# Two heads in flight in a gated-delta block: the next head's projection written ahead of a head's chain, and small copies and sums on ScalarE

## The chip, the cores and the metric

The kernel runs on one core of a Trainium2 chip. The metric is the device time of one execution in microseconds (us), the median of several runs. The core has five engines that run their own instruction streams in order and wait for each other by semaphores: TensorE (PE in the rows, its weight loads PEld), VectorE (DVE), ScalarE (ACT), GpSimd (POOL) and SyncE (SP), which issues most DMAs.

## What is computed

A decoder trunk on x of 512 tokens by 1024, with two layers, conditioned by a vector c. The first layer mixes tokens with a gated delta rule in 8 heads of 128, then an MLP; the second makes a shared key and value, and does differential attention and another MLP. The change lies in the first layer's mixer, cut here to what matters:

```
def gated_deltanet(h, w_in, conv_w, a_log, dt_bias, out_g, w_out):
    proj = h @ w_in
    qkv = causal_conv_silu(proj[..., :2 * GDN_HK + GDN_HV], conv_w)     # 4 taps along the tokens
    ...
    o = gated_delta_rule(l2norm(q), l2norm(k), v, g, beta)
    o = rmsnorm(o, out_g) * jax.nn.silu(z)
    return o.reshape(B, S, GDN_HV) @ w_out

def gated_delta_rule(q, k, v, g, beta):   # in chunks
    a_mat = jnp.where(strict, jnp.einsum('bhnik,bhnjk->bhnij', kb, kc) * decay, 0.0)
    rhs = jnp.concatenate([vc * bc[..., None], kb * jnp.exp(gcum)[..., None]], axis=-1)
    sol = lax.linalg.triangular_solve(eye + a_mat, rhs, left_side=True, lower=True, unit_diagonal=True)
    ...
    def step(state, inp):
        v_new = u_i - jnp.einsum('bhck,bhkv->bhcv', w_i, state)
        o_i = jnp.einsum('bhck,bhkv->bhcv', qg_i, state) + jnp.einsum('bhij,bhjv->bhiv', qk_i, v_new)
        state = state * gl_i[..., None, None] + jnp.einsum('bhck,bhcv->bhkv', kd_i, v_new)
        return state, o_i
    _, o = lax.scan(step, s0, xs)
```

## The kernel before

The program is written in a tile framework. It names tiles and pools, and a scheduler turns the written order into one queue for each engine: of what is ready by its model, what was written earlier goes first. So the order of the Python code is a priority, and the queue that results is fixed when the program is built. Names in the rows are those of tiles; `pj`, `pa`, `pi`, `pr` are PSUM banks.

A head h of the mixer has two parts. `proj_head(h)` streams the weights of its q, k and v (L291, `raw`), rounds them on ScalarE to `wh` (L293), takes the remainder `wl` (L284), multiplies three times for each block (L300 to L302, 512 wide), and convolves the result in the tile `cv` (L481 to L485, one pass on ScalarE, three on VectorE, and the SiLU). `gdn(h)` is a generator in three pieces. The first makes the gate's decay (L531, L532), the natural layouts by transposes (L513), the scaled matrix `bq` (L558), and solves it: 16x16 blocks on 32 partitions in fifteen steps on VectorE (L584 and L586, tiles `pr` and `xv`); a DMA to DRAM and back lays the blocks out over 128 partitions (`tc`), from which VectorE makes `t` (L593). TensorE transposes t (L598) to z and doubles the inverse up to 128 in three rounds (L605 to L638), with `um` between (L607 for blocks of 16, L624 for 32 and 64). The second piece is the chain over four chunks of 128 tokens (L670 to L690), where each chunk has `y` (L681), then the state `st`, the residual `r` (L676) of the next chunk, and so on. The third piece normalizes the output `o` (L696 to L702), transposes it (L513) and scales it to `oT` (L705).

For each head, `proj_head(h)` is written first, then two pieces of `gdn(h)`, then the last piece of the head before it. After the eight heads come the gate's projections (L717, L719, in four pairs of heads), the last piece of head 7, the rounding of `oT` (L745, L284) and the output projection. Spread over the weights tiles is a queue of products for the modulation vectors (L189 loads `mw`, L193 multiplies on VectorE), with MWB buffers.

Three sums of squares in each head (`sumsq`, L518 and L520, of k, q and o) are a Square of 128x512 on ScalarE, then a reduction on VectorE.

Of the kernel before, what the change touches and what calls it, by code (L numbers as in the profile page):

```python
# [12 lines left out]
AF = mybir.ActivationFunctionType  # L13
ALU = mybir.AluOpType
AX = mybir.AxisListType
# [6 lines left out]
NT = S // P  # L22
H = 8
# [8 lines left out]
PAD, PAD_W, PAD_R = 416, 0, 96  # L32
MB = 8
AHEAD = 2
MWB = 4
NE = (0, 1, 2, 1, 2, 0, 1, 0)
CV = 9


C_MODB = 0  # L40
# [45 lines left out]
def trunk_kernel(ctx: ExitStack, tc: tile.TileContext, a, outT):  # L86
    nc = tc.nc
    V, G, A, T = nc.vector, nc.gpsimd, nc.scalar, nc.tensor
# [3 lines left out]
    def nm(s):  # L92
        count[0] += 1
        return f"{s}_{count[0]}"

    def open_pool(name, side="left", bufs=1):
        st = ExitStack()
        p = st.enter_context(tc.tile_pool(name=nm(name), bufs=bufs, side=side, reuse_waits="tile"))
        return p, st
# [28 lines left out]
    def big(pool, tag, bufs, dt=F32):  # L128
        return pool.tile([P, S], dt, tag=tag, name=nm(tag), bufs=bufs)

    def col(n, name="c"):
        return tp.tile([P, n], F32, tag=f"{name}{n}", name=nm(name))

    def bank(tag):
        return pools["p"].tile([P, S], F32, tag=tag, name=nm("p" + tag), bufs=pools["n"][tag])
# [4 lines left out]
    def v3(ap, n=P):  # L140
        return ap.rearrange("p (u f) -> p u f", f=n)
# [34 lines left out]
    def cc(base, n=1):  # L176
        return cols[:, base:base + n]
# [7 lines left out]

    def mod_load(c, pool=None, bufs=MWB):
        src = a["mod_wT"][c * P:(c + 1) * P, :] if c < 96 else a["kv_mod_wT"][(c - 96) * P:(c - 95) * P, :]
        w = (pool or c_pool).tile([P, D], F32, tag="mw", name=nm("mw"), bufs=bufs)
        nc.sync.dma_start(w, src)  # L189
        return w  # L190
# [182 lines left out]
    for k in range(KT):  # L373
        n = NE[k]
        sq = acc[n]
        if k >= 3:
            sq = m_pool.tile([P, S], F32, tag=f"sq{n}", name=nm("sq"), bufs=2)
# [17 lines left out]
    def head_weights(h, k0):  # L395
        return weights(lambda t: [(t[:, :, i, :], v_in[:, k0:k0 + 2, i, h * P:(h + 1) * P]) for i in range(3)],
                       [2, 3, P])

    def head_pair(ps, w, k0):
        for j in (1, 0, 2):  # L400
            for k in range(2):
                three(ps[j], w[0][:, k, j], w[1][:, k, j], hh[k0 + k], hl[k0 + k], k0 + k == 0, k0 + k == KT - 1)
# [25 lines left out]
    g_pool, g_st = open_pool("g", "right")  # L428
# [48 lines left out]
    def conv_silu(ps, tile_idx):  # L477

        w = C_CONV + 4 * tile_idx
        acc = big(g_pool, "cv", CV)  # L480
        A.activation(acc, ps, AF.Copy, scale=cc(w + 3))  # L481
        for s in (1, 2, 3):
            V.scalar_tensor_tensor(out=acc[:, s:], in0=ps[:, :S - s], scalar=cc(w + 3 - s), in1=acc[:, s:],
                                   op0=ALU.mult, op1=ALU.add)
        A.activation(acc, acc, AF.Silu)  # L485
        return acc
# [3 lines left out]
    def proj_head(h):  # L490
        if h < 2:
            ps = ph[h]
        else:
            ps = [bank("j") for _ in range(3)]
            for k0 in range(0, KT, 2):
                head_pair(ps, head_weights(h, k0), k0)
        kT[h] = conv_silu(ps[1], 8 + h)
        qT[h] = conv_silu(ps[0], h)
        vT[h] = conv_silu(ps[2], 16 + h)

    def uu(t, n):
        return t[:, n * P:(n + 1) * P]
# [6 lines left out]
    def gdn(h):  # L509
# [4 lines left out]
            return ps  # L514

        def sumsq(src, tag):
            sq = big(g_pool, {"sqq": "sqk"}.get(tag, tag), 1)
            A.activation(sq, src, AF.Square)  # L518
            ss = col(4, tag)
            V.tensor_reduce(out=ss, in_=v3(sq), axis=AX.X, op=ALU.add)  # L520
            return ss


# [14 lines left out]
        kn = big(g_pool, "kn", 3)  # L538
        A.activation(kn, pk, AF.Copy)
        ssk = sumsq(kn, "sqk")  # L540
        V.tensor_scalar(out=ssk, in0=ssk, scalar1=EPS, scalar2=None, op0=ALU.add)
        rk = col(4, "rk")
# [18 lines left out]
        def B(n):  # L561
            return bq[n // 2][:, (n % 2) * 256:(n % 2) * 256 + P]

        def ATT(n):
            return bq[n // 2][:, (n % 2) * 256 + P:(n % 2) * 256 + 256]
# [16 lines left out]
        for s in range(SUB - 1):  # L582
# [4 lines left out]
                            op=ALU.subtract)  # L587
# [15 lines left out]
        pu = bank("i")  # L603
        for n in range(4):
            T.matmul(uu(pu, n), lhsT=B(n), rhs=uu(t_, n), start=True, stop=True)  # L605
        um = big(g_pool, "um", 1)
# [9 lines left out]
        for b in (32, 64):  # L616
            parts = [(slice(lo, lo + b), slice(lo + b, lo + 2 * b)) for lo in ((0, 64) if b == 32 else (0,))]
            pu = bank("i")
            um = big(g_pool, "um", 1)
            for p0, p1 in parts:  # L620
                for n in range(4):
                    T.matmul(pu[p1, n * b:(n + 1) * b], lhsT=B(n)[p0, p1], rhs=uu(t_, n)[p0, p0], start=True, stop=True)
            for p0, p1 in parts:
                V.tensor_copy(um[p1, 0:4 * b], pu[p1, 0:4 * b])  # L624
            pz = bank("i")
            for p0, p1 in parts:
                for n in range(4):
                    T.matmul(pz[p0, n * b:(n + 1) * b], lhsT=um[p1, n * b:(n + 1) * b], rhs=uu(z, n)[p1, p1],
                             start=True, stop=True)
            if b == 32:  # L630
                p0, p1 = parts[0]
                for n in range(4):
                    T.matmul(pz[p1, n * b:(n + 1) * b], lhsT=uu(z, n)[p1, p1], rhs=um[p1, n * b:(n + 1) * b],
                             start=True, stop=True)
                V.tensor_tensor(out=v3(t_)[p1, :, p0], in0=v3(t_)[p1, :, p0],
                                in1=v3(pz[p1, 0:4 * b], b), op=ALU.subtract)
            for p0, p1 in parts:
                V.tensor_tensor(out=v3(z)[p0, :, p1], in0=v3(z)[p0, :, p1], in1=v3(pz[p0, 0:4 * b], b),  # L638
                                op=ALU.subtract)
# [8 lines left out]
        V.tensor_tensor(out=v3(vn), in0=v3(pv), in1=bc(nk, P), op=ALU.mult)  # L648

        ssq = sumsq(natural(qT[h]), "sqq")  # L650
        V.tensor_scalar(out=ssq, in0=ssq, scalar1=float(P), scalar2=EPS * P, op0=ALU.mult, op1=ALU.add)
        rq = col(4, "rq")
# [6 lines left out]
        def out(c):  # L659
            V.tensor_tensor(out=uu(o, c), in0=uu(o, c), in1=R(2), op=ALU.add)  # L660
# [3 lines left out]
        def R(n):  # L664
            return ps[:, n * P:(n + 1) * P]

        for c in range(NT):
            r = uu(vn, 0)
            if c > 0:
                T.matmul(R(3), lhsT=uu(kT[h], c), rhs=st, start=True, stop=True)  # L670
                if c > 1:
                    out(c - 1)
                else:
                    A.activation(uu(o, 0), R(2), AF.Copy)
                r = g_pool.tile([P, P], F32, tag="r", name=nm("r"), bufs=2)
                V.scalar_tensor_tensor(out=r, in0=R(3), scalar=neg[:, c, h:h + 1], in1=uu(vn, c),  # L676
                                       op0=ALU.mult, op1=ALU.add)
                T.matmul(R(1), lhsT=uu(qT[h], c), rhs=st, start=True, stop=True)
            T.matmul(R(2), lhsT=uu(z, c), rhs=r, start=True, stop=True)
            y = g_pool.tile([P, P], F32, tag="y", name=nm("y"), bufs=2)  # L680
            V.tensor_copy(y, R(2))  # L681
            if c < NT - 1:
                T.matmul(R(0), lhsT=uu(kn, c), rhs=y, start=True, stop=True)
            T.matmul(R(2), lhsT=ATT(c), rhs=y, start=True, stop=True)
            if c > 0:
                A.activation(uu(o, c), R(1), AF.Copy, scale=eg[:, c, h:h + 1])
            if c == 0:
                V.tensor_copy(st, R(0))
            elif c < NT - 1:
                V.scalar_tensor_tensor(out=st, in0=st, scalar=gl[:, c, h:h + 1], in1=R(0), op0=ALU.mult, op1=ALU.add)  # L690
        out(NT - 1)

        yield

        so = sumsq(o, "sqo")
        V.tensor_tensor(out=so, in0=so, in1=rq, op=ALU.mult)  # L696
        V.tensor_tensor(out=so, in0=so, in1=rq, op=ALU.mult)
# [14 lines left out]
    def gate(h0, n):  # L712
        ps = proj_T(cols_of(w_in, 3072 + P * h0, P * n), KT, hh, hl, ntile=n)
        for j in range(n):
            h = h0 + j
            sz[h] = big(g_pool, "cv", CV)
            A.activation(sz[h], ps[j], AF.Silu)  # L717
# [8 lines left out]
        queue[c - 17][1].insert(0, lambda c=c: mod_bias(c - 8, c))  # L726
    rate[0] = 0.5
    heads = []
    for h in range(H):
        proj_head(h)  # L730
        heads.append(gdn(h))
        next(heads[h])
        next(heads[h])
        if h:
            next(heads[h - 1], None)
# [275 lines left out]
```

## Time and profile before

| What | Value |
|---|---|
| Median of 3 runs | 1383.1 us (1381.0 to 1383.88) |
| The profiled execution's own time | 1381.92 us |
| Its span in the trace | 1380.1 us |
| TensorE matmul, busy | 1309.7 us, 95% of the span |
| VectorE busy | 850.9 us, 62% |
| ScalarE busy | 529.1 us, 38% |
| GpSimd busy | 471.4 us, 34% |
| Mean granted clock of TensorE | 0.986 of full speed |
| Head 0's first transposes of t (L598) | at 130.2 us |
| Head 7's | at 355.7 us |
| Head 7's output transposes (L513) | at 391.8 us |
| First matmul of the norm behind the mixer | at 416.6 us |

Busy means that an instruction of the engine is running; a wide matmul's end is modelled, so a busy TensorE need not be at its peak. The rows below are from the one execution that was profiled. The last four lines of the table cut the mixer into the stretches that the rows use.

### The profile page before, as it was taken

What the parts mean: (1) busy time and instruction counts of PE and PEld (TensorE: products, weight loads), DVE (VectorE), ACT (ScalarE), POOL (GpSimd) and SP (SyncE); (2) the same over time, 40 slices, a digit from 0 to 9 for tenths busy, and PEclk for the clock granted to TensorE, in tenths of its full rate; (3) what the DMA queues carried; (4) which work ended last, traced back from release to release, by engine and by line L of the source; (5) the groups of instructions that cost most, each with busy time, mean ns of one, the idle gap of its engine ahead of it and who ended that gap; (6) DMA issues with size and microseconds to landing.
All of it is one profiled execution on the core that took longest, in us unless ns stands there. A gap on an engine that the chain in (4) does not pass through costs nothing. (4 is left out here: it accounts for less than half of the span.)

```text
span 1380.1 us, 19204 instructions
## 1 busy us (share of the span) xinstructions
PE 1309.7 (95%) x7240; PEld 1101.4 (80%) x7240; DVE 850.9 (62%) x1688; ACT 529.1 (38%) x951; POOL 471.4 (34%) x281
## 2 busy tenths in 40 slices
PE   4887998999999999999999999999999999999997
PEld 3665787777789888888888987888798888888886
DVE  6989899899846987778861687777552110031113
ACT  3394344443424533225332354444344322143221
POOL 3324132222004544444444012232135444444441
PEclk9997999999999999999999999999999999999998
DMA  9632223225542776776753233222113233233221
GB/s 314 212 90 57 81 78 81 74 72 147 175 151 65 266 239 225 242 236 219 241 165 100 81 100 104 65 66 66 61 62 123 92 96 103 92 100 99 92 76 62
DMA packets 113212, 174.97 MB, mean 127 GB/s; under 512 B 16384, under 2 KB 56992, under 8 KB 113120
## 3 DMA queue, kind: packets, MB, share of 16 engines
q1 hardware_dynamic: 112416, 172.92, 39.5%
q8 instruction: 57, 0.93, 0.3%
q10 hardware_dynamic: 704, 0.83, 0.2%
q14 instruction: 35, 0.29, 0.1%
HBM read 170.04 MB, written 2.62 MB: 125 GB/s over the span
## 5 line engine op out<-in xcount | busy, mean ns | idle before, releaser
L284 POOL TENSOR_TENSOR wl<-raw,wh 128x1024 fp32r<-128x1024 f32 (+1 forms) x137 | 329.3, 2404 | 392.9 <-ACT wh L293 392.9
L293 ACT ACTIVATE wh<-raw 128x1024 fp32r<-128x1024 f32 (+2 forms) x217 | 216.0, 996 | 502.0 <-PE pj L301 250.1
L300 PE MATMUL pj<-h,wh 128*128 128x512 f32 (+1 forms) x816 | 290.9, 360 | 16.0 <-ACT h L278 5.5
L301 PE MATMUL pj<-h,wh 128*128 128x512 f32 (+1 forms) x816 | 292.6, 359 | 0.0
L302 PE MATMUL pj<-h,wl 128*128 128x512 f32 (+1 forms) x816 | 290.4, 358 | 1.1 <-DVE wl L284 1.1
L193 DVE SCALAR_TENSOR_TENSOR mw<-mw,one,cs 128x1024 f32<-128x1024 f32 x96 | 210.1, 2202 | 47.5 <-ACT one L213 47.2
L300 PEld LDWEIGHTS pj<-h,wh 128*128 128x128 f32 x816 | 155.9, 192 | 37.2 <-ACT h L278 7.5
L302 PEld LDWEIGHTS pj<-h,wl 128*128 128x128 f32 x816 | 156.6, 192 | 19.4 <-DVE wl L284 2.4
L301 PEld LDWEIGHTS pj<-h,wh 128*128 128x128 f32 x816 | 156.9, 192 | 17.9 <-DVE h L279 0.3
L301 PE MATMUL pj<-u,wh 128*128 128x512 f32 (+1 forms) x448 | 160.9, 359 | 0.0
L302 PE MATMUL pj<-u,wl 128*128 128x512 f32 (+1 forms) x448 | 160.9, 359 | 0.0
L300 PE MATMUL pj<-u,wh 128*128 128x512 f32 (+1 forms) x448 | 160.8, 359 | 0.0
L346 DVE SCALAR_TENSOR_TENSOR x<-pj,mod,x 128x256 f32<-128x256 f32 (+1 forms) x53 | 30.2, 584 | 152.2 <-PE pj L302 152.2
L284 DVE TENSOR_TENSOR wl<-raw,wh 128x1024 fp32r<-128x1024 f32 (+2 forms) x80 | 84.5, 1058 | 18.7 <-ACT wh L293 18.6
L300 PEld LDWEIGHTS pj<-u,wh 128*128 128x128 f32 x448 | 84.6, 189 | 12.7 <-issue 0.2
L301 PEld LDWEIGHTS pj<-u,wh 128*128 128x128 f32 x448 | 84.6, 189 | 12.5
L302 PEld LDWEIGHTS pj<-u,wl 128*128 128x128 f32 x448 | 84.6, 189 | 12.5
L767 DVE SCALAR_TENSOR_TENSOR pj<-pj,r 128x512 f32<-128x512 f32 x32 | 21.6, 690 | 52.2 <-ACT r L766 52.0
L301 PE MATMUL pn<-h,wh 128*128 128x512 f32 x128 | 49.8, 389 | 0.0
L300 PE MATMUL pn<-h,wh 128*128 128x512 f32 x128 | 49.8, 389 | 0.0
L300 PE MATMUL pm<-h,wh 128*128 128x512 f32 x128 | 49.8, 389 | 0.0
L302 PE MATMUL pm<-h,wl 128*128 128x512 f32 x128 | 49.8, 389 | 0.0
(298 smaller groups left out, 2371.7 us busy)
## 6 DMA issues: line engine op xcount, KB each, us to landing
raw<-in_mlp_w_dram SPq DMA_DIRECT2D x128, 512.0 KB, 3.7
mw<-in_mod_wT_dram SPq DMA_DIRECT2D x96, 512.0 KB, 4.7
raw<-in_a_w_in_dram SPq DMA_DIRECT2D x96, 128.0 KB, 2.6
mw<-in_kv_mod_wT_dram SPq DMA_DIRECT2D x16, 512.0 KB, 5.1
raw<-in_kv_w_dram SPq DMA_DIRECT2D x16, 512.0 KB, 3.3
x<-in_xT_dram SPq DMA_DIRECT2D x16, 256.0 KB, 6.0
raw<-in_a_w_in_dram SPq DMA_DIRECT2D x16, 256.0 KB, 2.9
raw<-in_a_w_out_dram SPq DMA_DIRECT2D x8, 512.0 KB, 4.3
```

Of the source, the lines that this page charges most:

```text
L193: V.scalar_tensor_tensor(out=w, in0=w, scalar=one, in1=cs, op0=ALU.mult, op1=ALU.mult, accum_out=raw_mod[:, c:c + 1])
L284: (V if n else G).tensor_tensor(out=out, in0=x, in1=hi.bitcast(F32), op=ALU.subtract)
L293: A.activation(wh, raw, AF.Copy)
L300: T.matmul(ps, lhsT=wh, rhs=xh, start=first, stop=False, skip_group_check=skip)
L301: T.matmul(ps, lhsT=wh, rhs=xl, start=False, stop=False, skip_group_check=skip)
L302: T.matmul(ps, lhsT=wl, rhs=xh, start=False, stop=last, skip_group_check=skip)
L346: V.scalar_tensor_tensor(out=x[d][:, sl], in0=ps[j][:, sl], scalar=mod[:, gt + d:gt + d + 1], in1=x[d][:, sl], op0=ALU.mult, op1=ALU.add)
L767: V.scalar_tensor_tensor(out=ps[j], in0=ps[j], scalar=0.0, in1=r, op0=ALU.max, op1=ALU.mult)
```

## The change

There are four edits. `proj_head(h + 1)` is now written ahead of `gdn(h)`, so that two heads' q, k and v are held (CV, the buffers of `cv`, goes from 9 to 12, and MWB from 4 to 3). `sumsq` uses four Squares of 128x128 with an accumulator on ScalarE in place of one of 128x512 and a reduction on VectorE. The copies of `um` for blocks of 32 and 64 and those of `y` move from VectorE to ScalarE.

```
-MWB = 4
+MWB = 3
-CV = 9
+CV = 12
...
         def sumsq(src, tag):
-            sq = big(g_pool, {"sqq": "sqk"}.get(tag, tag), 1)
-            A.activation(sq, src, AF.Square)
+            sq = big(g_pool, "sqk", 1)
             ss = col(4, tag)
-            V.tensor_reduce(out=ss, in_=v3(sq), axis=AX.X, op=ALU.add)
+            for c in range(NT):
+                A.activation(uu(sq, c), uu(src, c), AF.Square, accum_out=ss[:, c:c + 1])
             return ss
...
             for p0, p1 in parts:
-                V.tensor_copy(um[p1, 0:4 * b], pu[p1, 0:4 * b])
+                A.activation(um[p1, 0:4 * b], pu[p1, 0:4 * b], AF.Copy)
...
             y = g_pool.tile([P, P], F32, tag="y", name=nm("y"), bufs=2)
-            V.tensor_copy(y, R(2))
+            A.activation(y, R(2), AF.Copy)
...
     heads = []
+    proj_head(0)
     for h in range(H):
-        proj_head(h)
+        if h + 1 < H:
+            proj_head(h + 1)
         heads.append(gdn(h))
         next(heads[h])
         next(heads[h])
```

The queues that the scheduler makes of both programs show where work goes. On TensorE, at the first work on head 7's inverse (L598 of its tile `t`), before had projections of 512 columns (`pj`) between the steps:

```order
L598 MATMUL pi_3231<-mask,t_3229 128x128 x4
L605 MATMUL pi_3238<-t_3229,bq_3167 128x128 x2
L605 MATMUL pi_3238<-t_3229,bq_3168 128x128 x2
L300 MATMUL pj_3656<-h_170,wh_3659 128x512
L301 MATMUL pj_3656<-h_171,wh_3659 128x512
L302 MATMUL pj_3656<-h_170,wl_3661 128x512
L300 MATMUL pj_3655<-h_172,wh_3677 128x512
L301 MATMUL pj_3655<-h_173,wh_3677 128x512
L610 MATMUL pi_3245<-um_3243,z_3236 128x128 x4
L613 MATMUL pi_3250<-z_3236,um_3243 128x128 x4
L302 MATMUL pj_3655<-h_172,wl_3679 128x512
L300 MATMUL pj_3655<-h_174,wh_3677 128x512
```

In the changed program the same steps of head 7 follow one another, behind the last of these projections:

```order
L301 MATMUL pa_3849<-h_3825,wh_3922 128x512
L302 MATMUL pa_3849<-h_3824,wl_3924 128x512
L598 MATMUL pi_3273<-mask,t_3271 128x128 x4
L605 MATMUL pi_3280<-t_3271,bq_3209 128x128 x2
L605 MATMUL pi_3280<-t_3271,bq_3210 128x128 x2
L610 MATMUL pi_3287<-um_3285,z_3278 128x128 x4
L613 MATMUL pi_3292<-z_3278,um_3285 128x128 x4
L622 MATMUL pi_3299<-t_3271,bq_3209 32x32 x2
L622 MATMUL pi_3299<-t_3271,bq_3210 32x32 x2
L622 MATMUL pi_3299<-t_3271,bq_3209 32x32 x2
L622 MATMUL pi_3299<-t_3271,bq_3210 32x32 x2
```

The projections that stood among head 7's steps are ahead of L598. Counted over the whole queue, 512-wide matmuls ahead of head 0's L598 (from the first solve step on) go from 54 to 113, between head 0's and head 7's from 489 to 541, from there to head 7's output transposes from 94 to 0, and behind these, up to the MLP, from 41 to 24.

On VectorE, the stretch up to head 7's `t` (L593) in the program before, with the chain of head 6 ahead of it (`y_2979`, `sqo_3368`):

```order
L284 TENSOR_TENSOR wl_3702<-raw_3698,wh_3700 128x512
L681 COPY y_2979<-pr_2942 128x128
L660 TENSOR_TENSOR o_2941<-o_2941,pr_2942 128x128
L719 TENSOR_TENSOR x_2613<-cv_3649,x_2613 128x512
L520 TENSOR_REDUCE sqo_3368<-sqo_3366 128x4
L696 TENSOR_TENSOR sqo_3368<-sqo_3368,rq_2938 128x4
L697 TENSOR_TENSOR sqo_3368<-sqo_3368,rq_2938 128x4
L698 TENSOR_SCALAR sqo_3368<-sqo_3368 128x4
L284 TENSOR_TENSOR wl_3720<-raw_3716,wh_3718 128x512
L593 TENSOR_TENSOR t_3229<-tc_3227,mask 128x512
L701 TENSOR_TENSOR ro_3373<-ro_3373,rq_2938 128x4
```

And in the changed program, where the steps of head 7's own solve (`xv_3234`) come last before `t_3271`:

```order
L584 TENSOR_TENSOR pr_3235<-mt_3232,xv_3234 32x2x14
L586 TENSOR_TENSOR xv_3234<-xv_3234,pr_3235 32x2x14
L284 TENSOR_TENSOR wl_4041<-raw_4037,wh_4039 128x1024
L584 TENSOR_TENSOR pr_3235<-mt_3232,xv_3234 32x15
L586 TENSOR_TENSOR xv_3234<-xv_3234,pr_3235 32x15
L284 TENSOR_TENSOR wl_4047<-raw_4043,wh_4045 128x1024
L593 TENSOR_TENSOR t_3271<-tc_3269,mask 128x512
L607 TENSOR_TENSOR um_3285<-pi_3280,mask 128x512
L614 TENSOR_TENSOR t_3271<-t_3271,pi_3287 128x512
L615 TENSOR_TENSOR z_3278<-z_3278,pi_3292 128x512
```

The last solve step of head 7 now stands one instruction ahead of its `t`, with the remainder of a weight (`wl`) between.

On ScalarE, in the first head's chain, the program before has roundings of weights (`wh`), the `cv` of the next head, and the outputs of the chain (`o`):

```order
L600 ACTIVATE z_692<-pi_687 128x512
L293 ACTIVATE wh_1862<-raw_1858 128x768
L293 ACTIVATE wh_1888<-raw_1884 128x768
L213 ACTIVATE one_1892<-wh_1888 128x1
L293 ACTIVATE wh_1919<-raw_1915 128x768
L481 ACTIVATE cv_1590<-pj_1474,cols 128x512
L674 ACTIVATE o_779<-pr_780 128x128
L481 ACTIVATE cv_1596<-pj_1473,cols 128x512
L293 ACTIVATE wh_1945<-raw_1941 128x768
L686 ACTIVATE o_779<-pr_780,eg_all 128x128
```

In the changed program the copies `um` and `y` of the same head stand among them, with the Squares of its sum of squares (`sqo_1217`):

```order
L624 ACTIVATE um_734<-pi_733 32x128 x2
L293 ACTIVATE wh_2019<-raw_2015 128x768
L624 ACTIVATE um_762<-pi_761 64x256
L681 ACTIVATE y_804<-pr_802 128x128
L293 ACTIVATE wh_2045<-raw_2041 128x768
L213 ACTIVATE one_2049<-wh_2045 128x1
L674 ACTIVATE o_801<-pr_802 128x128
L520 ACTIVATE sqk_1216,sqo_1217<-o_801 128x128
L681 ACTIVATE y_815<-pr_802 128x128
L686 ACTIVATE o_801<-pr_802,eg_all 128x128
```

The copies and the squares are new in this queue, and each stands behind whatever rounding precedes it. Of 48 rows with moved copies in the whole queue, 10 follow a rounding directly (a row with x2 holds two copies).

## Rows read from the trace of the kernel before

**Rows 1.** Busy time of each engine, granted clock and DMA share by stretch (us).
```profile
core 0: us, PE busy (x) PEld busy (x) DVE busy (x) ACT busy (x) POOL busy (x), PEclk, DMA share, GB/s
86.00:130.00 44.00, 33.35 (x146) 25.67 (x145) 37.35 (x115) 28.05 (x52) 18.25 (x17) 0.81 0.21 55
130.00:355.70 225.70, 213.61 (x1488) 173.81 (x1488) 199.59 (x595) 95.77 (x176) 55.66 (x42) 0.98 0.35 95
355.70:391.80 36.10, 33.14 (x216) 26.24 (x216) 28.69 (x55) 14.45 (x25) 4.24 (x3) 1.00 0.50 159
391.80:416.60 24.80, 24.79 (x157) 22.67 (x158) 12.16 (x20) 6.61 (x11) 0.00 (x0) 0.93 0.45 150
100.00:120.00 20.00, 14.62 (x60) 11.16 (x59) 18.72 (x53) 11.97 (x21) 10.68 (x9) 0.67 0.05 8
500.00:520.00 20.00, 20.00 (x90) 16.58 (x89) 16.42 (x18) 8.28 (x15) 7.28 (x4) 1.00 0.69 229
```

**Rows 2.** Waits of TensorE, 130 to 355.7 us: total, times, longest; ten rows.
```profile
PE pi L598 <- DVE t L593: 5.5, 4, 2.6
...
PE pr L683 <- DVE y L681: 0.2, 1, 0.2
```

**Rows 3.** VectorE groups, 84 to 400 us: busy, mean ns, idle before.
```profile
L193 DVE SCALAR_TENSOR_TENSOR mw<-mw,one,cs 128x1024 f32<-128x1024 f32 x24 | 31.3, 1303 | 0.0
L284 DVE TENSOR_TENSOR wl<-raw,wh 128x768 fp32r<-128x768 f32 x22 | 22.3, 1016 | 0.0
...
L483 DVE SCALAR_TENSOR_TENSOR cv<-pj,cols,cv 128x510 f32<-128x510 f32 x18 | 13.2, 734 | 0.1
...
L681 DVE COPY y<-pr 128x128 f32<-128x128 f32 x32 | 9.0, 283 | 2.8 <-PE pr L679 2.5
...
L520 DVE TENSOR_REDUCE sqo<-sqo 128x4 f32<-128x512 f32 x8 | 5.4, 678 | 1.2 <-ACT sqo L518 1.1
...
L624 DVE COPY um<-pi 32x128 f32<-32x128 f32 x16 | 4.6, 290 | 3.0 <-PE pi L622 2.6
...
L624 DVE COPY um<-pi 64x256 f32<-64x256 f32 x8 | 3.4, 428 | 6.7 <-PE pi L622 6.7
```

**Rows 4.** ScalarE groups, 84 to 400 us, the same columns.
```profile
L518 ACT ACTIVATE sqk<-kn 128x512 f32<-128x512 f32 x8 | 5.0, 624 | 0.1
...
L674 ACT ACTIVATE o<-pr 128x128 f32<-128x128 f32 x8 | 2.2, 275 | 15.1 <-PE pr L670 15.1
```

**Rows 5.** ScalarE's reads of an accumulator in the attention, 860 to 980 us.
```profile
L914 ACT ACTIVATION_READ_ACCUMULATOR on<-po 128x1 f32 x16 | 3.2, 199 | 0.0
```

**Rows 6.** Timeline of TensorE: start us, length us, and idle before.
```profile
155.94 1.06 PE L613 MATMUL pi<-z,um 128*128 128x128 f32 x8
...
391.81 0.66 PE L513 MATMUL pr<-mask,o 128*128 128x128 f32 x4 [2.39 <-POOL o L702]
```

**Rows 7.** Timeline of VectorE, the same columns.
```profile
182.78 0.67 DVE L593 TENSOR_TENSOR t<-tc,mask 128x512 f32<-128x512 f32 x1
...
195.90 0.29 DVE L681 COPY y<-pr 128x128 f32<-128x128 f32 x1
...
306.99 0.27 DVE L681 COPY y<-pr 128x128 f32<-128x128 f32 x1
...
310.60 0.28 DVE L681 COPY y<-pr 128x128 f32<-128x128 f32 x1
...
354.85 0.69 DVE L593 TENSOR_TENSOR t<-tc,mask 128x512 f32<-128x512 f32 x1 [0.72 <-DMA tc<-d]
...
384.30 0.29 DVE L681 COPY y<-pr 128x128 f32<-128x128 f32 x1 [0.82 <-PE pr L679]
```

**Rows 8.** What SyncE's DMA queue waited for, whole span.
```profile
SPq L189 <- DVE mw L193: 88.8, 69, 6.7
```

**Rows 9.** Waits of ScalarE, 84 to 400 us: total, times, longest.
```profile
ACT wh L293 <- PE pj L301: 38.7, 17, 5.2
...
ACT wh L293 <- DMA raw<-in_a_w_in_dram: 24.7, 9, 4.5
```

## The prediction

> **What bounds the kernel now.** I looked first at the share of each engine by stretch, because the change touches only the recurrent block, from 86 us (its first solve step is near) to 416.6 us (the first work of the MLP) [rows 1]. TensorE is busy for 33.35 of 44.00 us before head 0's inverse reaches it (I call this the start), for 213.61 of 225.70 us from head 0's to head 7's (the middle), for 33.14 of 36.10 us in head 7's own chain (the last chain), and for 24.79 of 24.80 us in what is left behind it (the flush). So the block is TensorE's: its queue is long enough that the chains of the heads hide under projection. VectorE is the next one, with 37.35, 199.59 and 28.69 us in the first three stretches. ScalarE has room, with 144.9 us in all four.
>
> The second view is the list of what TensorE waits for in the middle: ten rows from 5.5 to 0.2 us, which add up to 14.3 us [rows 2]. The largest, four waits of 5.5 us together, is for t, the first tile that the solve gives to TensorE; the wait for y is 0.2 us. A faster VectorE can give back in the middle no more than these 14.3 us, whatever is taken from it.
>
> The amount of TensorE's work does not change: both programs issue the same matmuls. What can change is where they stand, thus how much idle time each stretch holds.
>
> **What leaves VectorE and comes to ScalarE.** VectorE loses 32 copies of y (9.0 us), 24 reductions of about 0.68 us (16.3 us) and 24 copies of um (4.6 and 3.4 us), 33.3 us in all [rows 3]. ScalarE gains the copies at its own price for such a tile, 32 x 0.275 = 8.8 us and about 7 us for um. A sum of squares was one pass of 0.624 us there [rows 4]; it becomes four passes of about 0.28, each with a read of the accumulator. Before has such a read elsewhere, at 0.199 us [rows 5], so four passes are 1.9 us, 1.28 more, and 24 of them 30.7 us. ScalarE goes to about 191 of 330 us. A copy takes as long on the one engine as on the other (0.283 and 0.275), so the chain is not shorter by it; only the queue ahead of it differs. I take nothing for that (bounds: a gain up to the 0.2 us wait for y and a loss, which is a rival below).
>
> **The start.** By the order of instructions TensorE has 59 more 512-wide matmuls ahead of head 0's inverse (54 before, 113 now), since head 1's projection stands there, and 8 transposes fewer. One such matmul costs 20.00/90 = 0.222 us in a full stretch [rows 1], a transpose of one block 0.13, as a share of eight fp32 passes of that size in 1.06 us [rows 6]. So TensorE's work in the start is 33.35 + 13.1 - 1.1 = 45.4 us, 1.4 more than the whole stretch of 44.00: the lower bound, +1.4, if no idle is left. VectorE's queue there gains five convolution steps of 0.73, four weight remainders of 1.02 and two modulation products of 1.30 (10.3 us), and loses three reductions (2.0 us) [rows 3]: +8.3 as the upper bound. The order shows that four scalings, six solve steps and three reductions or masks of 0.2 to 1.0 us each also leave it. That takes another 5.5 us or so, an estimate from their number, and I take +2.8.
>
> **The middle.** Between the two inverses the order has 52 more 512-wide matmuls (489 before, 541 now), 8 more transposes and 2 more small matmuls of the decay: 11.5 + 1.1 + 0.4 = 13.0 us. Against it stand the waits of 14.3 us. VectorE's queue from t to t loses 33 us but gains nine weight remainders, three modulation products and the scalings moved in from the start, 198 to 189 us by the same prices. Thus VectorE and TensorE stay near each other head by head, and what TensorE waits for is mostly t. Head 7's t itself waited 0.72 us for a DMA [rows 7], the round trip by which the solved blocks are spread over the partitions. In the new order the solve's last step stands only one instruction ahead of t on VectorE, so this trip is exposed rather than covered. Bounds for the waits that remain: 2 us (all but the transfers vanish) and 14.3 (nothing gained). I take 12, near the upper end, because the largest row ends on a chain through a DMA that no freed VectorE shortens. The middle then gives 13.0 - 2.3 = +10.7.
>
> **The last chain.** Here the cover goes. Before, 94 matmuls of 512 stand in TensorE's queue in it; now none does, and the 72 output matmuls that do not need the last heads stand ahead of head 7's inverse. What is left is the bare chain. Its length I build from the fastest pieces in the trace [rows 7]: t to the first y is 13.1 us for head 2 (182.78 to 195.90), y to the next y 3.6 (306.99 to 310.60), and the last y of head 7 to its output transposes 7.5 (384.30, and 391.81 in [rows 6], which contains 2.39 us of waiting for GpSimd). 13.1 + 3 x 3.6 + 7.5 = 31.4 from t, 30.5 from the inverse, which is 0.85 later; the reduction that goes takes 0.7 from it. Even these pieces were stretched by work in between, so 26 is the lower bound. The upper bound is 33: where TensorE was busy for only 14.62 of 20 us its granted clock was 0.67 [rows 1], between the two levels, and the chain's small matmuls would run longer. I take 30 against 36.1: -6.1.
>
> **The flush.** 17 matmuls fewer stand there (41 before, 24 now): -3.8. But the last head's tile must now be rounded and its remainder taken with little else in front: two passes over 128x512, 0.62 [rows 4] and 0.69 [rows 7], about +1.4. Sum -2.4.
>
> **The smaller edits.** Three modulation buffers in place of four: at four, the queue of loads already waits in 69 places for VectorE to free one, 88.8 us [rows 8]. Those waits are hidden because TensorE runs without any gap in the MLP, 20.00 of 20.00 us [rows 1]. Nothing; if the cover failed, each product that came late would be queued on VectorE with a wait of at most 6.7 us. Twelve buffers for the convolution instead of nine is what lets two heads be in flight; it costs no time.
>
> **Sum:** 2.8 + 10.7 - 6.1 - 2.4 = +5.0 on the profiled execution's own 1381.92, that is 1386.9. The median of the runs lies 1.2 above that execution, so 1388.
>
> **A rule against this.** TensorE's matmul busy time overstates how full it is, if one follows the Trainium skill, "Perfetto Trace Analysis", section "Identifying the Most-Contended Engine": it judges TensorE by the busy share of its weight loads and the others by occupancy. By this VectorE (265.6 us in the first three stretches) leads over the weight loads (225.7), and the page's section "Optimizing Scalar/DVE Operations" says that offloading to ScalarE may make sense when VectorE is saturated. By it the whole 33 us less some overlap would come back, about -27, or 1356; the row of waits, which allows at most 14.3 us, speaks against it.
>
> **The rivals.**
> (a) Faster: the cover lost at the end was worth less, and the waits in the middle vanish as VectorE is relieved. Waits to 2 and a last chain of 27: 2.8 + 13.0 - 12.3 - 9.1 - 2.4 = -8.0, or 1375. For it: nine tenths of the middle's waits name VectorE. Against: t's waits are the end of a chain. It decides once the chain is below 28 us and the waits below 6. Chance 0.24.
> (b) VectorE is what really holds TensorE, also where no wait shows: 1356, as above, by taking back most of 33 us. Chance 0.04.
> (c) About no change: waits of 7 us and a chain of 29 give 2.8 + 13.0 - 7.3 - 7.1 - 2.4 = -1.0, or 1382. The change then only moves idle time from the start to the end. Chance 0.20.
> (d) Slower still: the copies on ScalarE are caught behind a rounding of weights that waits. ScalarE waited 17 times for TensorE to free a weight buffer (38.7 us) and 9 times for the weights (24.7 us) [rows 9], 2.4 us each, in about 26 of 44 roundings. In the new order 10 of the 48 rows of moved copies stand right behind a rounding. 10 x 26/44 x 2.4 = 14 us, of which TensorE, in order behind y, would feel between half and all: 1395 to 1402. It decides if more than two of those ten wait. Against it: the buffer is freed by matmuls that stand ahead of y's reader on TensorE, so most waits end early. Chance 0.12.
> The forecast, slower by 3 to 9 us (own range 1386 to 1393), has 0.40.
>
> About 0.2%, or 2.8 us, is what measurement can tell from no change here. (a) and (b) are faster, 0.28; (c) is the same, 0.20; the forecast and (d) are slower, 0.52. The range from 1373 to 1401 leaves out (b) and the ends of (a) and (d), some 0.15 to 0.2.
>
> **What the new profile would show.** Right: TensorE nearly gapless from 86 us until head 7's inverse, which comes later than 355.7 (near 369); then a last chain of about 30 us with TensorE busy for well under half and a lower granted clock; a flush of some 22 us; VectorE lower by some 33 us in the block, ScalarE up by 47. The waits for t remain at the head of TensorE's list in the middle. Wrong: a head 7 inverse at or before 362 means that the waits in the middle were VectorE's load, (a). A new wait of TensorE for ScalarE's y or um of 10 us or more means (d). A last chain below 27 or above 33 us means that its pieces were misjudged. A change in the MLP's span by more than 1 us would contradict the cover claimed for three buffers.

## The result, and the profile after

The changed kernel takes 1392.7 us (median of 4 runs, 1391.6 to 1394.3), the kernel before 1383.4 beside it. The ratio is 1.0072, with a 95% interval of 1.0054 to 1.0089: slower by 0.7%, or 9.3 us. The profiled execution took 1393.15 us, 11.2 more than that of before.

The same stretches as in [rows 1], cut at the same events (head 0's inverse, head 7's inverse, head 7's output, the first work of the MLP), with one more row for all that follows:

```profile
core 0: us, PE busy (x) PEld busy (x) DVE busy (x) ACT busy (x) POOL busy (x), PEclk, DMA share, GB/s
86.00:131.00 45.00, 40.81 (x198) 32.11 (x199) 37.59 (x108) 31.20 (x80) 18.22 (x13) 0.95 0.40 111
131.00:375.60 244.60, 229.74 (x1550) 182.85 (x1549) 200.17 (x555) 130.85 (x377) 48.46 (x46) 0.99 0.37 103
375.60:406.40 30.80, 18.58 (x122) 14.18 (x122) 7.29 (x21) 6.93 (x22) 2.36 (x2) 0.64 0.21 69
406.40:429.40 23.00, 21.99 (x141) 19.93 (x142) 11.05 (x19) 5.55 (x10) 0.00 (x0) 0.89 0.14 46
429.40:1391.00 961.60, 943.98 (x4996) 805.79 (x4994) 500.65 (x794) 345.92 (x634) 368.27 (x200) 1.00 0.39 127
```

Read the second number of each row against [rows 1]. The start is 1.0 us longer, although TensorE is busy in it for 7.5 us more: its idle time there fell from 10.65 to 4.19. The middle is longer by 18.9 us. The last chain is shorter by 5.3 but nearly bare, with 12.2 us idle and a granted clock of 0.64, between its two levels. The flush is 1.8 shorter. What follows takes 1.4 us less. So the middle is the stretch that got longer: TensorE's busy time grew there by 16.1 us, and its idle time by another 2.8 (12.1 to 14.9). Much of that busy time is work that stood in the last chain before, so the lengths alone do not say where time was lost. TensorE's idle time over the four stretches went from 25.7 to 32.3 us: 6.5 less in the start, 2.8 more in the middle, 9.3 more in the last chain and 1.0 more in the flush. Its busy time went from 304.9 to 311.1, for the same matmuls.

TensorE's waits in the middle, to set beside [rows 2] (us in total, times, longest), and head 7's wait for t, which falls just behind the window's end:

```profile
PE pi L598 <- DVE t L593: 3.2, 2, 2.4
PE pa L513 <- DVE bq L558: 2.9, 1, 2.9
PE pa L513 <- DVE pr L584: 1.9, 1, 1.9
...
375.61 0.63 PE L598 MATMUL pi<-mask,t 128*128 128x128 f32 x4 [2.87 <-DVE t L593]
```

The nine rows of that list add up to 11.9 us, and head 7's 2.9 makes 14.8, against 14.3 before. So relieving VectorE won nothing back in this list. No row names y or um on ScalarE.

What ScalarE got (the Square is now on L520), to set beside [rows 3] to [rows 5]:

```profile
L520 ACT ACTIVATE sqk<-kn 128x128 f32<-128x128 f32 x32 | 9.5, 301 | 0.1
L681 ACT ACTIVATE y<-pr 128x128 f32<-128x128 f32 x32 | 8.8, 275 | 28.2 <-PE pr L679 26.2 <-DVE pr L584 1.3 <-DVE xv L586 0.7
...
L520 ACT ACTIVATION_READ_ACCUMULATOR sqk<-kn 128x1 f32 x32 | 6.1, 191 | 0.0
```

The view that explains the middle is the order on ScalarE. In the kernel before, k's squares of head 7 (`sqk<-kn`, the beginning of its gate, its scaled matrix and its solve) come 25 us ahead of the squares of head 5's output (`sqo<-o`); the first and the last row are head 0's and head 7's output, for the pace of the heads:

```profile
161.24 0.61 ACT L518 ACTIVATE sqo<-o 128x512 f32<-128x512 f32 x1
...
297.57 0.63 ACT L518 ACTIVATE sqk<-kn 128x512 f32<-128x512 f32 x1
...
322.55 0.61 ACT L518 ACTIVATE sqo<-o 128x512 f32<-128x512 f32 x1
...
385.93 0.63 ACT L518 ACTIVATE sqo<-o 128x512 f32<-128x512 f32 x1 [0.35 <-DVE o L660]
```

In the changed kernel they come right behind the last of these:

```profile
156.58 0.31 ACT L520 ACTIVATE sqk<-o 128x128 f32<-128x128 f32 x1
...
323.61 0.31 ACT L520 ACTIVATE sqk<-o 128x128 f32<-128x128 f32 x1
...
324.04 0.31 ACT L520 ACTIVATE sqk<-kn 128x128 f32<-128x128 f32 x1
...
402.54 0.31 ACT L520 ACTIVATE sqk<-o 128x128 f32<-128x128 f32 x1 [0.35 <-DVE o L660]
```

It is so for each of the heads 2 to 7, by 0.4 to 1.6 us. Both squares are now written to one tile, `sqk`, as the line `sq = big(g_pool, "sqk", 1)` of the diff says; before, o's had a tile of their own. In the program's text k's squares of head h+2 stand behind o's squares of head h, so with a single buffer k's squares of head h+2, and the gate, the scaled matrix and the solve that need them, can't begin before head h's chain has ended. This edit is not among the four named in the section on the change. From head 0's output to head 7's it is 224.7 us before and 246.0 now, or 32.1 and 35.1 per head.

### The profile page after: what moved, and what is told of

Same layout as the page of the kernel before. It is cut to its first block, busy times and chain, and to the rows that moved or that the text cites. A ratio compares the mean times of both kernels' runs of the same rounds, so it can differ in the third digit from the quotient of the medians.

```text
span 1391.4 us, 19379 instructions
## 1 busy us (share of the span) xinstructions
PE 1313.8 (94%) x7240; PEld 1100.5 (79%) x7240; DVE 827.9 (60%) x1608; ACT 558.8 (40%) x1175; POOL 463.6 (33%) x281
## 5 line engine op out<-in xcount | busy, mean ns | idle before, releaser
L193 DVE SCALAR_TENSOR_TENSOR mw<-mw,one,cs 128x1024 f32<-128x1024 f32 x96 | 206.8, 2166 | 51.7 <-ACT one L213 49.9
L284 DVE TENSOR_TENSOR wl<-raw,wh 128x1024 fp32r<-128x1024 f32 (+2 forms) x80 | 83.8, 1049 | 21.7 <-ACT wh L293 21.3
L301 PEld LDWEIGHTS pj<-u,wh 128*128 128x128 f32 x448 | 84.6, 189 | 12.6
L302 PE MATMUL pn<-h,wl 128*128 128x512 f32 x128 | 49.8, 389 | 0.0
```

The source lines that it names most:

```text
L193: V.scalar_tensor_tensor(out=w, in0=w, scalar=one, in1=cs, op0=ALU.mult, op1=ALU.mult, accum_out=raw_mod[:, c:c + 1])
L284: (V if n else G).tensor_tensor(out=out, in0=x, in1=hi.bitcast(F32), op=ALU.subtract)
L301: T.matmul(ps, lhsT=wh, rhs=xl, start=False, stop=False, skip_group_check=skip)
L302: T.matmul(ps, lhsT=wl, rhs=xh, start=False, stop=last, skip_group_check=skip)
```

## The experiments

There were three batches of four, in the order of the table, each timed in turn with the kernel before on one chip (the third batch on another chip than the first two). The median of the kernel before was 1382.8 to 1385.0 us in them, so the ratio is the fair comparison.

| Kernel | us | ratio to before (95%) |
|---|---|---|
| order_only | 1420.1 | 1.0259 (1.0240 to 1.0278) |
| sums_only | 1413.6 | 1.0210 (1.0192 to 1.0229) |
| copies_only | 1380.3 | 0.9965 (0.9952 to 0.9978) |
| cover2 | 1398.9 | 1.0100 (1.0082 to 1.0117) |
| tile_shared | 1427.7 | 1.0323 (1.0303 to 1.0342) |
| all_own_tile | 1374.5 | 0.9932 (0.9919 to 0.9946) |
| scalar_own_tile | 1371.1 | 0.9909 (0.9896 to 0.9923) |
| order_own_tile | 1380.1 | 0.9978 (0.9968 to 0.9988) |
| q_o_share | 1372.2 | 0.9907 (0.9882 to 0.9933) |
| changed_cv11 | 1396.2 | 1.0082 (1.0063 to 1.0101) |
| sums_own_tile | 1367.0 | 0.9875 (0.9854 to 0.9896) |
| mwb3_only | 1383.2 | 0.9998 (0.9985 to 1.0010) |

### The change in three parts, and a cover put back

**order_only** is the changed kernel with the reductions and copies back on VectorE (it keeps the one tile for squares):

```
-            for c in range(NT):
-                A.activation(uu(sq, c), uu(src, c), AF.Square, accum_out=ss[:, c:c + 1])
+            A.activation(sq, src, AF.Square)
+            V.tensor_reduce(out=ss, in_=v3(sq), axis=AX.X, op=ALU.add)
...
+                V.tensor_copy(um[p1, 0:4 * b], pu[p1, 0:4 * b])
...
+            V.tensor_copy(y, R(2))
```

> The next head's projection is written ahead (with MWB 3, CV 12 and one tile for the squares), and the reductions and the copies of um and y stay on VectorE. Theory A (what counts is where the 512-wide matmuls stand: 852 of the 888 that I count stand ahead of head 7's inverse, 15 in its chain, 21 behind, against 864, 0 and 24 in the changed kernel and 753, 94 and 41 in the one before): about the time of the changed kernel, 1390 to 1395 us, with a last chain of 30 to 32 us. Rival B (the order is harmless or helps, and the loss comes from ScalarE's new work): at most 1384. Rival C (VectorE's relief holds the loss of the order down): 1400 or more.

**sums_only** is the kernel before with the new `sumsq`, its tile included, and nothing else.

> The kernel before with nothing but the sums of squares by accumulators on ScalarE. Its queue on TensorE has 864 matmuls of 512 ahead of head 7's inverse and none in its chain, just as the changed kernel, without the new order of heads. Theory A: 1388 to 1395, with a bare last chain of about 31 us. Rival (only the new order of heads takes the cover away): 1383 or less.

**copies_only** is the kernel before with the two lines of um and y.

> The kernel before with nothing but the copies of um and y on ScalarE. Its queue has 714 matmuls of 512 ahead of head 7's inverse, 92 in the last chain and 82 behind it. Theory A: total unchanged, 1381 to 1387, with the inverse of head 7 near 346 us, a chain of 36 and a flush of 34. Rival (copies caught on ScalarE behind roundings that wait): 1392 or more, with TensorE waiting for y or um by 10 us or more.

**cover2** is the changed kernel, where the weights of the last two gates are rounded with a factor of one made from head 7's t:

```
+            tie[0] = col(1, "tie")
+            A.activation(tie[0], tof[H - 1][:, 0:1], AF.Copy, scale=0.0, bias=1.0)
...
-        A.activation(wh, raw, AF.Copy)
+            A.activation(wh, raw, AF.Copy, scale=tie[0])
```

> The changed kernel, where the weights of the last pair of gate projections are rounded with a factor of one that is made from head 7's t, so that these 48 matmuls and what follows them can't stand ahead of head 7's inverse: 744 stand ahead of it, 82 in its chain, 62 behind. Theory A in its simple form (the bare last chain costs 12 us of idle, and work put there is free): 1380 to 1384, with a last chain that has under 3 us of idle. Rival (TensorE's cover is conserved: what is moved into the last chain is missing between the inverses of heads 6 and 7, which then has only 4 matmuls): 1388 to 1396, with a new idle time of 8 us or more in that stretch.

The copies came out as theory A had it (inverse of head 7 at 345.3 us, a chain of 35.7, a flush of 32.7), save that the total lies just under its range: 0.35% faster, where no change was expected. Nothing else did. Each of order_only and sums_only alone lost about three to four times what the whole change loses. Theory A, that the time follows from where the 512-wide matmuls stand, fell: sums_only has the same count ahead of head 7's inverse as the changed kernel and is some 19 us slower (1.0210 against 1.0072). Rival B of order_only and the rival of sums_only (that one part alone is harmless) fell too. Rival C of order_only, that relief of VectorE holds a loss down, fits order_only, but not sums_only, where VectorE is relieved as well.

cover2 showed that the empty last chain is not by itself what costs: its rival had it right, though the time came out 3 us above the rival's. Its last chain of 41.9 us has 36.1 us of TensorE's work, but the idle time turned up ahead of head 7's inverse, at a low clock (a window over parts of the chains of heads 5 and 6):

```profile
300.00:360.00 60.00, 47.07 (x323) 36.59 (x321) 35.19 (x125) 21.42 (x74) 10.80 (x10) 0.78 0.09 22
```

So something other than TensorE's queue sets when head 7's inverse can be had. What order_only and sums_only share with the changed kernel, and copies_only does not, is the one tile for squares.

### The tile

**tile_shared** is the kernel before with that one edit. No instruction is added or removed:

```
-            sq = big(g_pool, {"sqq": "sqk"}.get(tag, tag), 1)
+            sq = big(g_pool, "sqk", 1)
```

> The kernel before with one edit: the squares of q, k and o share one tile of one buffer (the tag sqk for all three); before, o's squares had a tile of their own. No operation is added or taken away. Since k's squares of head h+2 are written after o's squares of head h, they can only be made once head h's chain has ended. Theory T (this wait, and not the work on ScalarE or the order of heads, is what takes the cover from the last heads: in this queue 852 matmuls of 512 stand ahead of head 7's inverse and 15 in its chain, against 753 and 94): 1405 to 1425 us. Rival (a tile more or less for scratch is nothing): within 3 us of the kernel before.

**all_own_tile** is the changed kernel with that line as it was before, and CV 11 to make room.

> The changed kernel with o's squares in a tile of their own again (CV is 11 in place of 12, to make room). 746 matmuls stand ahead of head 7's inverse, 84 in its chain, 58 behind it; heads are still written one ahead. Theory T: 1370 to 1382, faster than both, with under 6 us of idle in the last chain. Rival (writing the heads ahead empties the last chain whatever the tile, and VectorE's relief gives nothing): 1388 or more.

**scalar_own_tile** has all three moves to ScalarE with the old line, and the order of heads, CV and MWB of before.

> The kernel before with all three moves to ScalarE (sums, um, y), the tile of o's squares kept apart, and its own order of heads, CV 9 and MWB 4. Theory T: 1370 to 1382, as the moves relieve VectorE and the cover is kept (713 ahead of head 7's inverse, 85 in its chain, 90 behind). Rival (the sums on ScalarE cost more than they give, as each is 1.3 us longer there): 1384 to 1392.

**order_own_tile** is order_only with the old line and CV 11.

> The heads written one ahead, nothing moved to ScalarE, o's squares in a tile of their own, CV 11, MWB 3. Against order_only, which was at 1420, the tile and one buffer of cv are all that differs. Theory T: 1380 to 1390. Rival (without relief of VectorE the order of heads is what costs 35 us): 1405 or more.

All four went as theory T had it, tile_shared just beyond its range: one scratch tile less costs 3.2%, 44 us, by itself. No instruction differs, only the order in the queues that the scheduler makes of the new dependency: by the count in the expectation, 99 more of the 512-wide matmuls stand ahead of head 7's inverse. ScalarE's timeline there shows head 4's output squared, then VectorE reducing it, and only then k of head 6 (the first and last row are again head 0's and head 7's output, 39.8 us per head):

```profile
161.92 0.63 ACT L518 ACTIVATE sqk<-o 128x512 f32<-128x512 f32 x1 [0.35 <-DVE o L660]
...
328.27 0.63 ACT L518 ACTIVATE sqk<-o 128x512 f32<-128x512 f32 x1 [0.35 <-DVE o L660]
...
332.39 0.63 ACT L518 ACTIVATE sqk<-kn 128x512 f32<-128x512 f32 x1 [2.51 <-DVE sqo L520]
...
440.45 0.63 ACT L518 ACTIVATE sqk<-o 128x512 f32<-128x512 f32 x1 [0.35 <-DVE o L660]
```

With its tile back, the changed kernel has k's squares of head 7 ahead of o's of head 5 again, and the heads' outputs come 31.0 us apart:

```profile
157.90 0.31 ACT L520 ACTIVATE sqo<-o 128x128 f32<-128x128 f32 x1 [0.99 <-DVE o L660]
...
298.86 0.29 ACT L520 ACTIVATE sqk<-kn 128x128 f32<-128x128 f32 x1
...
304.11 0.29 ACT L520 ACTIVATE sqo<-o 128x128 f32<-128x128 f32 x1
...
315.35 0.31 ACT L520 ACTIVATE sqo<-o 128x128 f32<-128x128 f32 x1 [0.35 <-DVE o L660]
...
374.78 0.31 ACT L520 ACTIVATE sqo<-o 128x128 f32<-128x128 f32 x1 [0.39 <-DVE o L660]
```

and the block (from 84 us to the first work of the MLP) shrinks. The first row is all_own_tile, the second tile_shared, the third scalar_own_tile; TensorE's busy time is in them for the same matmuls:

```profile
84.00:408.50 324.50, 305.12 (x2017) 246.14 (x2016) 254.91 (x705) 174.94 (x490) 73.84 (x62) 0.97 0.36 103
```

```profile
84.00:466.60 382.60, 331.89 (x2018) 269.11 (x2017) 286.40 (x785) 147.19 (x266) 77.39 (x62) 0.88 0.30 88
```

```profile
84.00:405.90 321.90, 302.54 (x2016) 242.61 (x2016) 258.75 (x705) 175.51 (x490) 78.25 (x62) 0.98 0.36 104
```

Idle time is 19.4, 50.7 and 19.4 us (length less TensorE's busy time), against 25.9 for the kernel before and 32.3 for the changed one in the same stretch. Busy time times granted clock is 296, 292 and 296 us, so the busy time differs with the clock, which was 0.88 in tile_shared, where TensorE is idle most.

### Is it the tile, the room, or which squares wait?

**q_o_share** has two tiles again, but q's squares share one with o's:

```
-            sq = big(g_pool, "sqk", 1)
+            sq = big(g_pool, {"sqq": "sqo"}.get(tag, tag), 1)
```

> The changed kernel with two tiles for squares, where k has its own and q shares one with o (CV 11). The number of tiles and the room are those of all_own_tile; a wait of head h+2 for head h's output is still there, but on q's squares, which only the final norm needs, not on k's, from which the solve starts. Theory T (it is the wait of k's squares that costs): within 4 us of all_own_tile, 1371 to 1379. Rival (any tie between the heads costs, or the number of tiles alone): 1385 or more, or (if CV 11 were what helps) this can't be told from the next run.

**changed_cv11** is the control for the buffers.

> The changed kernel with CV 11 in place of 12 and nothing else: the part of all_own_tile that is not the tile. Theory T: 1389 to 1397, as the changed kernel. Rival (one cv buffer fewer holds projections back for the last chain, and this made all_own_tile fast): 1380 or less.

**sums_own_tile** is sums_only with the old line for the tile.

> The kernel before with only the sums of squares by accumulators on ScalarE, and o's squares in their own tile. If the moves add up, it is copies_only's distance from the scalar_own_tile run: 1371.1 + (1383.5 - 1380.3), about 1374 (1371 to 1378). Rival (the sums are worth nothing without the copies): 1381 or more. Theory T excludes only a time as that of sums_only, 1414.

**mwb3_only** has `MWB = 3` and nothing else.

> The kernel before with three modulation buffers in place of four. Its queues are the same. The prediction's step says nothing, within 2.8 us of 1383.5; the rival (a product that comes late holds up VectorE) 1387 or more.

q_o_share is as fast as all_own_tile, though its q now shares a tile with o just as k did. In its timeline `sqo<-pa` is q of a later head, and follows the last of o at once (within about 1 us, as for three more of the six heads); k is long done:

```profile
299.81 0.29 ACT L520 ACTIVATE sqk<-kn 128x128 f32<-128x128 f32 x1
...
316.30 0.31 ACT L520 ACTIVATE sqo<-o 128x128 f32<-128x128 f32 x1 [0.35 <-DVE o L660]
316.74 0.28 ACT L520 ACTIVATE sqo<-pa 128x128 f32<-128x128 f32 x1
```

So it is not that there is a tie between heads, but which squares are tied: k stands at the head of the solve. changed_cv11 is as slow as the changed kernel, so the buffer of cv did nothing for all_own_tile, and the tile alone is 1.0082 to 0.9932, 1.5% or 21 us, of the changed kernel. These two kernels differ in the tile's line and nothing else, so their stretches show where it costs. The first two rows are the middle and the last chain of changed_cv11, the other two those of all_own_tile:

```profile
129.70:377.80 248.10, 231.50 (x1549) 182.44 (x1550) 198.27 (x556) 127.88 (x374) 48.95 (x46) 0.98 0.36 102
377.80:408.60 30.80, 18.53 (x123) 14.19 (x123) 8.32 (x22) 6.93 (x22) 2.36 (x2) 0.64 0.21 69
129.50:340.30 210.80, 199.89 (x1400) 160.81 (x1400) 174.12 (x517) 113.41 (x339) 49.63 (x44) 0.97 0.32 90
340.30:378.70 38.40, 35.78 (x241) 28.34 (x239) 27.12 (x58) 20.46 (x55) 5.03 (x4) 1.00 0.49 157
```

With the shared tile 149 more matmuls stand in the middle and 118 fewer in the last chain. TensorE's idle time is 5.7 us longer in the middle and 9.7 in the last chain: the tile costs more as cover that is used up early than as waits in the middle.

The modulation buffers are nothing, as predicted. sums_own_tile, whose block has this row, was better than expected: the moves do not add up. The sums alone give 1367.0 (0.9875), with the copies 1371.1 (0.9909); the copies, which gain 0.35% by themselves, add nothing to the sums. That they cost something there is not shown, as the two intervals touch. The version with the sums alone beats both kernels, by 1.2% and (0.9875/1.0072) 2.0%.

```profile
84.00:400.00 316.00, 299.88 (x2017) 244.55 (x2017) 267.06 (x761) 160.99 (x434) 77.36 (x62) 0.98 0.37 106
```

## Why the prediction was right, and where it was not

The direction, the range and the way by which time was lost at the end of the block (a bare chain) were right. The cause was missing. The bare chain was read off the finished queue, in which the effect of the tile already stood, so its price came out nearly right without what made it. The size was less than half: +5.0 on the profiled execution, where 11.2 was measured. That 1392.7 still lies in the range of 1386 to 1393, by 0.3 us, is luck: the middle came out 8.2 us above its term, and the start and the MLP together 3.2 below.

**The middle, the step that failed.** The prediction put +10.7: 13.0 of added matmuls less 2.3 of waits. It was +18.9. TensorE's busy time rose by 16.1 in place of 13.0, or, with 1.5 for the small ones as predicted, (16.1 - 1.5)/52 = 0.28 for each added 512-wide matmul in place of 0.222. That price came from a stretch of nothing but such matmuls; why it is higher among short ones was not tested. And the idle time rose by 2.8 in place of falling by 2.3. The waits remained for t, as was said, but not because of the DMA behind the solve: VectorE was idle for that DMA ahead of t for 0.3 us in all heads together, against 1.4 before. The solve began late. The diff's line on the tile is not mentioned in the prediction; it stood in the sum at nothing, without a reason. It closes a loop: o's squares of head h, then k's of head h+2, its solve and chain, and o's squares of head h+2. Two such loops alternate. The runs are read here as follows: when a turn takes longer than TensorE needs for the work of two heads, the loop sets the pace, and the scheduler fills TensorE meanwhile with matmuls that would have covered the last chain. The pace fits this: 35.1 us per head in the changed kernel and 39.8 in tile_shared, where the reduction on VectorE stands in the loop as well, against 32.1 before and 31.0 in all_own_tile. Over all profiles it is 34.3 to 39.8 in the six kernels with the one tile, and 28.8 to 32.1 in the eight where o's squares are kept apart from k's. Seven heads by 35.1 - 32.1 are 21 us, about the 18.9 by which the middle got longer. Why the changed kernel loses less than sums_only or order_only, which have the same tile, was not taken apart further.

**The last chain.** -6.1 was forecast from a length of 30 us, and it took 30.8: -5.3. The pieces were less good than their sum. From t to the first y took 10.8 us (13.1 taken), the steps from y to y 5.0 (3.6 taken), from the last y to the output 5.8 (7.5). That no cover stands there was right, with 12.2 us idle; but cover2 shows that these 12 us are not free for the asking, and all_own_tile, that they shrink to 2.6 once the solve of head 7 is early.

**The start** was +1.0 (+2.8 forecast), under the lower bound of +1.4 that was drawn at before's clock: TensorE was granted 0.95 there in place of 0.81. At that clock the bound's own terms give 33.35 x 0.81/0.95 + 13.1 - 1.1, an estimate of about 40.4 us of work in place of 45.4, and 40.81 was measured. **The flush** was -1.8 (-2.4). **The MLP** and what follows are 1.4 us shorter, more than the 1 us that was set as its limit. That limit was too narrow: the same stretch took 960.9 to 965.1 us in the fourteen profiles, and all the kernels do the same work there. mwb3_only, at 0.9998, shows that three buffers in place of four cost nothing.

**ScalarE's load** rose by 29.7 us in the four stretches, not 47. A read of the accumulator takes 0.19 us but runs beside the next Square: the squares of k start 0.30 apart, so a sum is 1.2 us and not 1.9. VectorE's busy time fell by 21.7 us in these stretches, not by the 33 that its operations take one by one.

**The rivals.** (d), copies caught on ScalarE, did not come: no wait for y or um in the middle, and copies_only was faster. (c), about no change, did not come either. (a), 1375 us, is the time of all_own_tile, 1374.5, but not by (a)'s way, waits of 2 us and a last chain of 27: its last chain is 38.4 us long and covered, and its middle holds 10.9 us of idle time. (b), 27 us faster by relief of VectorE, did not come; with the tile apart the sums alone give 1.25%, some 17 us, and all three moves 12. Both show less idle time in the block (sums_own_tile 16.1 us, scalar_own_tile 19.4, before 25.9) and a higher granted clock (0.98 against 0.96). That it is VectorE's relief that gives this is not shown: sums_own_tile gains 17 us, where VectorE's busy time in the block fell by 12.6 (279.7 to 267.1), and its Squares of o also start chunk by chunk, ahead of the chain's end, which no run took apart. The rule of the Trainium skill, "Perfetto Trace Analysis", section "Optimizing Scalar/DVE Operations", is that offloading to ScalarE may make sense if VectorE is saturated. VectorE was busy for 84% of the four stretches before [rows 1], and the gain of these two runs agrees with the rule; in the change as it was written the tile hid it. That TensorE's matmul busy time overstates how full it is was the prediction's own reading of 280.1 us of matmul against 225.7 of weight loads in three stretches; no run tested it.

## What to carry to other kernels

When an edit lets two uses share a scratch buffer, treat it as a new wait: find which use comes first in the program's text, what it waits for, and what hangs on the other. Here one tile of 2 KB per partition cost 44 us. A loop over two iterations that closes through a buffer need not show in the list of TensorE's waits (14.3 us before, 14.8 in the changed kernel), since other work fills its queue in the meantime; it shows when the same event of each head is put side by side in both traces. And a part that costs much alone may cost less in company (the tile costs 44 us alone and 21 here), so a change is told apart by undoing single lines, not by adding up its parts.

## What the runs showed of the hardware that was not expected

Four Squares of 128x128 with an accumulator take ScalarE 1.2 us, as each read (0.19 us) overlaps the next Square. And a chain without other matmuls ran its steps from y to y in 5.0 us at a granted clock of 0.64, where the fastest step beside projections was 3.6 [rows 7]; whether the clock alone makes the difference was not tested.
